# Linear-attention keys of layer 1 in memory of their own, projected and scored ahead of the state-space mixer's end

## The chip, the cores and the metric

The kernel runs on one core of one Trainium2 chip, in one launch. The metric is the device time of one execution in microseconds (us), the median of several runs. In the profile PE is the tensor engine, DVE the vector engine, ACT the scalar engine, POOL the general engine and SP the engine whose queue issues the DMAs.

## The reference, cut to what matters

Two layers of a hybrid backbone act on 512 latent tokens and 256 context tokens (768 together, width 1024). In each layer a normalised input is projected once, and the result is cut into four head groups: A, a chunked gating MLP; B, bidirectional gated linear attention; C, a bidirectional state-space mixer (S5); D, latent attention with rotary positions. Their outputs are joined and projected back, and a gated feed-forward block follows. Only the latent tokens leave layer 1, so there the context rows matter only as keys, values and states.

Group B is the one whose work is moved:

```
q, k, v, g = rs(q), rs(k), rs(v), rs(g)          # chunks of 64 tokens
cum = jnp.cumsum(g, axis=2)
q_in = q * jnp.exp(cum)
k_in = k * jnp.exp(-cum)
scores = jnp.where(tri, einsum('bcthk,bcshk->bchts', q_in, k_in), 0.0)
o_intra = einsum('bchts,bcshv->bcthv', scores, v)
s_fin, s_start = lax.scan(step, s0, (decay, kv_chunk))   # state from chunk to chunk
o_inter = einsum('bcthk,bchkv->bcthv', q_in, s_start)
out = rmsnorm(o_intra + o_inter, g_norm) * silu(r)
```

## The kernel before, in words

Tokens lie along the free axis, features along the partitions. A float32 product is made of three matmuls on a high and a low part of each operand (`mm3`, lines 199 to 201). A weight block of 512 KB is loaded as `raw`, then ACT makes its high part `whi` (L191) and DVE its low part `wlo` (L192). The order on each engine is set by a scheduler that goes over the program; each engine works its own list off in order, and SP issues the DMAs in order too.

`mixers` writes one layer's mixers. The state-space mixer (`mixer_c`, lines 680 to 818) runs in a memory pool `mc`, and projections of the other groups run beside it, two at a time, in the accumulators `pg`; `evac` copies them out on ACT (L1536 for the latent part, L1538 for the context part). `heads` (L1565ff) projects q or k in two halves ("half 0", "half 1") and copies each head to the other 64 partitions by a DMA within the on-chip memory (L1572).

A pool's memory is given out as a stack. The keys (`bk`, 128 x 4 x 768) and the gate `r` (`rt`) live in pool `mb`, which is opened after `mc` is closed and so lies in `mc`'s memory: the first write of a key waits for the state-space mixer's last reader (L818).

`mixer_b` is a generator with stations: the gates (L845 to L868), the scaling of q (L873, L874), then in one station the scaling of k (L878 on ACT, L879 on DVE), six blocks of transposes of k (L885 on PE, copied by L886 on ACT), the scores (L897 on PE, masked by L901 and L902 on DVE), the state scan of 12 steps (L922 on PE, L929 to L932 on DVE, L912 and L913 on ACT) and the outputs (L944 to L957). Latent attention (`mixer_d`) follows with a rotated key part (L1088 on PE, which needs the table `dcst` loaded by L1068), values (L1097), projections (L1109, L1121) and attention.

In the state-space mixer of layer 1 the last part is: 96 matmuls in four groups (L786, L788) on 32 KB tables `s5t` (L680) and `s5e` (L781), copies (L789), a gelu (L792), transposes (L798), copies (L800), the gate product (L814, L816 to L818) and the store of its output (`dmixr<-s5a`, L1552).

Of the kernel before, what the change touches and what calls it, by code (L numbers as in the profile page):

```python
# [15 lines left out]
ALU = mybir.AluOpType  # L16
# [74 lines left out]
class Net:  # L91
# [730 lines left out]
    def mixer_b(self, l, e, gl, pg, psp, ctx_out):  # L822
# [14 lines left out]
        tmp = self.t(pg, [128, 2, T], "bsc")  # L837
# [3 lines left out]
        for hp in range(2):  # L841
            for h in (2 * hp, 2 * hp + 1):
                ps = self.t(self.psp, [128, 1024], p2)
# [3 lines left out]
                b = self.col(l, "bgate", h)  # L847
# [23 lines left out]
        tmp = self.t(pg, [128, 2, T], "bsc")  # L871
# [1 line left out]
            nc.scalar.activation(tmp[:, h % 2, :tn], gates[:, h, :tn], AF.Exp, scale=1.0 / 16)  # L873
            stt(qd[:, h, :tn], qd[:, h, :tn], 0.125, tmp[:, h % 2, :tn], op0=ALU.mult, op1=ALU.mult)  # L874
        yield
        p, kd, vt = e.p, e.k, e.v
        for h in range(4):
            nc.scalar.activation(tmp[:, h % 2], gates[:, h], AF.Exp, scale=-1.0 / 16)  # L878
            tt(kd[:, h], kd[:, h], tmp[:, h % 2], op=ALU.mult)  # L879

        ktok = self.t(pg, [128, 6, 4, 128], "bg")
        for i in (4, 5, 0, 3, 1, 2):
            ps = self.t(self.psp, [128, 512], p1)
            for h in range(4):
                nc.tensor.transpose(ps[:, h * 128:(h + 1) * 128], kd[:, h, i * 128:(i + 1) * 128], self.ident)  # L885
            nc.scalar.copy(ktok[:, i].rearrange("p h c -> p (h c)"), ps[:])  # L886


# [1 line left out]
        for i in range(0, ni, 2):  # L890
            ps = self.t(self.psp, [128, 2, 2, 4, 64], p2)
            for d in range(2):
                for j in range(2):
                    for h in range(4):
                        for cp in range(2):
                            cs = slice((i + j) * 128 + cp * 64, (i + j) * 128 + cp * 64 + 64)
                            nc.tensor.matmul(ps[cp * 64:cp * 64 + 64, d, j, h, :], kd[d * 64:d * 64 + 64, h, cs],  # L897
                                             qd[d * 64:d * 64 + 64, h, cs], start=True, stop=True)
            m2 = self.m2.unsqueeze(1).to_broadcast([128, 8, 64])
            scv = sc[:, i:i + 2].rearrange("p i h t -> p (i h) t")  # L900
            tt(scv, ps[:, 0].rearrange("p j h t -> p (j h) t"), m2, op=ALU.mult)  # L901
            nc.vector.copy_predicated(scv, self.mgt[:], ps[:, 1].rearrange("p j h t -> p (j h) t"))  # L902

        sh = self.t(p, [128, 12, 4, 64], "bk")
        nc.gpsimd.memset(sh[0:64, 8], 0.0)
# [2 lines left out]
        for k in range(12):  # L908
# [7 lines left out]
            if k % 2 == 0:  # L916
                ps = self.t(self.psp, [128, 512], p1)
            o = k % 2 * 256
            for d, c in ((0, c0), (1, c1)):
                cp = (c % 2) * 64  # L920
# [17 lines left out]
        for i0 in range(0, ni, 2):  # L938
            ps = self.t(self.psp, [128, 512], p1)
# [6 lines left out]
            for o, i, h, cp in blocks:  # L946
                c = 2 * i + cp
# [7 lines left out]
        rs = self.rsqrt_dve(p, ss[:, :4 * ni], 4 * ni, 1.0 / 64, "br")  # L955
# [3 lines left out]
        rt = e.r  # L959
# [4 lines left out]
        for hp in range(2):  # L964
# [3 lines left out]
            ps = self.t(self.psp, [128, 1024], p2)  # L968
# [542 lines left out]
    def mixers(self, l, ctx, md, early=None):  # L1511
        nc = self.nc
        G = (0, 1, 2) if ctx else (0, 1)
        G3 = (0, 1, 2)
        tn = T if ctx else NX
# [5 lines left out]
        def fm(wv, groups):  # L1521
            px = pc = None
            if 0 in groups:
                px = self.t(self.psg, [128, 512], "pg")
                self.gemm_fm(wv, KT, self.hrhs, px, None, [g for g in groups if g < 2])
            if 2 in groups:
                pc = self.t(self.psg, [128, 512], "pg")
                self.gemm_fm(wv, KT, self.hrhs, None, pc[:, :256], [2])
            return px, pc


        def half(n, i):
# [18 lines left out]
        def store(o, k, mix, t0=0):  # L1551
            nc.sync.dma_start(md[:, o + k, t0:tn], mix[:, t0:tn])  # L1552
# [9 lines left out]
        px_ = mxs.__enter__()  # L1562
        env = SimpleNamespace()

        def heads(n, x, groups):
            w = 256 * len(groups)
            for hp in range(2):
                px, pc = fm(half(n, hp), groups)
                for hr in range(2):
                    rs = slice(hr * 64, hr * 64 + 64)  # L1570
                    evac(x[rs, 2 * hp + hr], px, pc, rs)
                    nc.sync.dma_start(x[64 - hr * 64:128 - hr * 64, 2 * hp + hr, :w], x[rs, 2 * hp + hr, :w])  # L1572

        rest = iter(())

        def visit(n):
            for _ in range(n):
                next(rest, None)

        with self.pool("mc") as pm:  # L1580
            with self.behind(self.hlast if tables else None):
                for _ in tables or ():
                    pass
            self.mixer_c(l, self.uf[l], lambda k, t: store(4, k, t), pm, pcp, "pc1", ctx)
            if l == 0:
                rest = chain(*(self.mod_pair(p, self.gate) for p in (1, 2)))
            visit(2)
            x12 = self.t(px_, [128, 4, T], "x12")
            x6 = self.t(px_, [128, 1536], "x6")
            ut = x12[:, 0:2]  # L1590
            va = x12[:, 2:4].rearrange("p a t -> p (a t)").rearrange("p (i c) -> p i c", i=6)
            for i in range(2):
                px, pc = fm(half("ua", i), G)
                evac(ut[:, i], px, pc, func=AF.Gelu_apprx_tanh)
                visit(1)
            tmajor("va", G, lambda g, ps: nc.scalar.activation(
                va[:, 2 * g:2 * g + 2].rearrange("p i c -> p (i c)"), ps[:], AF.Gelu_apprx_tanh))
            visit(2)
            self.mixer_a(l, ut, va, x6, px_, "pb2", ctx)
            visit(2)  # L1600
            for k in range(2):
                store(0, k, ut[:, k])
            for i in range(2):
                px, pc = fm(half("cq", i), G3 if i else G)
                evac(cq[:, i], px, pc)
                visit(1)
            px, pc = fm(half("ck", 0), G3)
            evac(ck, px, pc)
            visit(2)
            if tabs:  # L1610
                tabs.__exit__(None, None, None)
            mgs = self.pool("mg", side="right")
            pg = mgs.__enter__()
            b = self.mixer_b(l, env, cq[:, 1], pg, ("pb2", "pb1"), ctx)
            next(b)
            visit(2)
            self.latent_norms(l, cq, ck, pg, "pb2", "pb1", ctx)
            visit(4)
            env.q = self.t(px_, [128, 4, T], "x12")
            heads("q", env.q, G)  # L1620
            next(b)
            env.v = vb = self.t(px_, [128, 6, 256], "x6")
            tmajor("vb", G3, lambda g, ps: nc.scalar.copy(
                vb[:, 2 * g:2 * g + 2].rearrange("p i c -> p (i c)"), ps[:]))
        pcs.__exit__(None, None, None)
        with self.pool("mb") as env.p:
            env.k = self.t(env.p, [128, 4, T], "bk")
            env.r = rt = self.t(env.p, [128, 2, T], "rt")
            heads("k", env.k, G3)
            next(b)  # L1630
            for hp in range(2):
                px, pc = fm(half("r", hp), G)
                evac(rt[:, hp], px, pc)
            next(b, None)
            for k in range(2):
                store(2, k, rt[:, k])
            psgs.__exit__(None, None, None)
            self.pe = None
            psds = self.pool("psd", space=PSUM, side="right")
            mds = self.pool("md", side="right")  # L1640
            pd, psd = mds.__enter__(), psds.__enter__()
            self.psd = {2: [(psd, "pd2")], 1: [(psd, "pd1")]}
            d = self.mixer_d(l, cq, ck, lambda k, t, t0: store(6, k, t, t0), pd, pg, ctx)
            next(d)
        mxs.__exit__(None, None, None)
        psls.__exit__(None, None, None)
        with self.pool("pse", space=PSUM) as pse, self.pool("me") as self.pe:
# [159 lines left out]
```

## Time and profile before

| | |
|---|---|
| three runs | 1907.22, 1909.77, 1914.28 us |
| median | 1909.77 us |
| the profiled execution's own time | 1912.24 us |
| span of the profile | 1910.4 us |
| mean granted clock of PE | 0.944 of full speed |
| PE busy | 1775.8 us (93%) |
| DVE busy | 1197.7 us (63%) |
| ACT busy | 776.7 us (41%) |
| POOL busy | 123.9 us (6%) |

The busy shares are averages over stages with different limits, so they say only that PE is the engine most in use. The time scale of all rows below is us from the start of the span. Layer 1's mixers take from about 1180 to 1450 of it, its feed-forward block what follows. "Idle before <- X" on a row is the time in which the engine waited for X. The clock is a share of 2.4 GHz: 1.00 is that level, 0.50 is 1.2 GHz, and values between are stretches with both.

### The profile page before, as it was taken

The numbers are of one execution on the slowest core, as the hardware profiler recorded it, in microseconds if no ns is written. First come the engines' busy times: TensorE is split into PE (matmuls) and PEld (weight loads), VectorE is DVE, ScalarE is ACT, GpSimd is POOL, SyncE is SP. The second block draws the span as 40 slices with busy tenths as digits, with TensorE's granted clock in tenths as the row PEclk, the third lists the DMA queues.
The fourth block names the chain that finished last, engine by engine and source line by source line (L and its number), as shares of the span: only waits on it lengthen the run. The fifth ranks groups of instructions, "written<-read, shape, count | busy, mean of one in ns | idle before, by whom it ended". The sixth has DMA issues, their size and how long they took to land.

```text
span 1910.4 us, 28205 instructions
## 1 busy us (share of the span) xinstructions
PE 1775.8 (93%) x11256; PEld 1515.4 (79%) x11256; DVE 1197.7 (63%) x2200; ACT 776.7 (41%) x1242; POOL 123.9 (6%) x142
## 2 busy tenths in 40 slices
PE   5899989899989899999999988997989999999996
PEld 2785677679977788888888886886668988888886
DVE  8866734664879853554885775683565765455555
ACT  2433454454753333322322344364444653333332
POOL 0000000000430000000000033000000310000002
PEclk7999998899999999999999988998889899999998
DMA  9457630015623342222564433323102523323341
GB/s 351 140 170 253 200 95 24 28 37 185 204 70 112 109 122 78 88 89 85 183 185 133 143 100 104 115 69 95 33 24 94 187 83 88 110 78 110 86 146 45
DMA packets 94386, 222.14 MB, mean 116 GB/s; under 512 B 10928, under 2 KB 41008, under 8 KB 93232
## 3 DMA queue, kind: packets, MB, share of 16 engines
q1 hardware_dynamic: 94256, 220.36, 37.0%
q8 instruction: 88, 1.44, 0.3%
q14 instruction: 42, 0.34, 0.1%
HBM read 193.35 MB, written 24.08 MB: 114 GB/s over the span
## 4 chain that ended last, share of the span: by engine, by line
PE 71%; DVE 11%; issue 9%; ACT 4%; DMA 2%; POOL 1%; SPq 0%; POOLq 0%; DVEq 0%; ACTq 0%
PE pf L199 16%; PE pf L200 16%; PE pf L201 16%; PE pg L199 3%; PE pg L201 3%; PE pg L200 3%; PE pb L243 1%; DVE wlo L192 1%; PE pd L1161 1%; PE pn L322 1%; DVE z L1215 1%; PE pc L714 1%; ACT whi L191 1%; DMA bk<-bk 1%; DVE nu L389 1%
## 5 line engine op out<-in xcount | busy, mean ns | idle before, releaser
L192 DVE TENSOR_TENSOR wlo<-raw,whi 128x1024 fp32r<-128x1024 f32 (+1 forms) x215 | 252.5, 1175 | 292.4 <-ACT whi L191 289.5
L191 ACT ACTIVATE whi<-raw 128x1024 fp32r<-128x1024 f32 (+1 forms) x215 | 217.4, 1011 | 398.0 <-PE pf L200 340.7
L199 PE MATMUL pf<-hhx,whi 128*128 128x512 f32 (+1 forms) x1032 | 365.8, 360 | 13.3 <-DVE z L1215 6.0
L200 PE MATMUL pf<-hlx,whi 128*128 128x512 f32 (+1 forms) x1032 | 369.1, 359 | 6.1 <-DVE hlx L391 5.9
L201 PE MATMUL pf<-hhx,wlo 128*128 128x512 f32 (+1 forms) x1032 | 366.8, 357 | 0.7 <-DVE wlo L192 0.5
L199 PEld LDWEIGHTS pf<-hhx,whi 128*128 128x128 f32 x1032 | 199.9, 196 | 41.2 <-issue 7.3
L200 PEld LDWEIGHTS pf<-hlx,whi 128*128 128x128 f32 x1032 | 201.8, 196 | 33.6 <-DVE hlx L391 8.9
L201 PEld LDWEIGHTS pf<-hhx,wlo 128*128 128x128 f32 x1032 | 201.8, 196 | 27.0 <-DVE wlo L192 1.5
L199 PE MATMUL pf<-g,whi 128*128 128x512 f32 (+1 forms) x552 | 185.8, 342 | 5.3 <-DVE z L1215 2.9
L201 PE MATMUL pf<-g,wlo 128*128 128x512 f32 (+1 forms) x552 | 187.5, 341 | 0.8 <-DVE wlo L192 0.8
L200 PE MATMUL pf<-g,whi 128*128 128x512 f32 (+1 forms) x552 | 187.8, 341 | 0.0
L1215 DVE SCALAR_TENSOR_TENSOR z<-pf,cols,z 128x511 f32<-128x511 f32 (+1 forms) x264 | 167.9, 656 | 28.3 <-ACT z L1213 25.8
L200 PE MATMUL pf<-hl,whi 128*128 128x256 f32 x432 | 123.0, 286 | 0.4 <-DVE hl L391 0.4
L199 PE MATMUL pf<-hh,whi 128*128 128x256 f32 x432 | 121.5, 286 | 1.6 <-ACT hh L390 1.5
L201 PE MATMUL pf<-hh,wlo 128*128 128x256 f32 x432 | 122.1, 284 | 0.0
L199 PEld LDWEIGHTS pf<-g,whi 128*128 128x128 f32 x552 | 104.7, 192 | 18.8 <-issue 3.7
L201 PEld LDWEIGHTS pf<-g,wlo 128*128 128x128 f32 x552 | 105.8, 192 | 12.2 <-DVE wlo L192 1.0
L200 PEld LDWEIGHTS pf<-g,whi 128*128 128x128 f32 x552 | 105.8, 192 | 11.5 <-DVE g L1265 0.2
L1213 ACT ACTIVATE z<-pf,cols 128x512 f32<-128x512 f32 (+1 forms) x132 | 90.1, 695 | 38.3 <-PE pf L201 29.9
L1294 DVE TENSOR_TENSOR y<-y,pf 128x512 f32<-128x512 f32 (+1 forms) x88 | 44.7, 515 | 73.1 <-PE pf L201 73.1
L125 POOL TENSOR_TENSOR nroy<-nroy,mhalf 128x2 f32<-128x2 f32 x10 | 10.0, 996 | 1202.4 <-DVE nroy L124 894.3
L199 PEld LDWEIGHTS pf<-hh,whi 128*128 128x128 f32 x432 | 82.4, 193 | 3.9 <-ACT hh L390 2.3
(465 smaller groups left out, 3408.5 us busy)
## 6 DMA issues: line engine op xcount, KB each, us to landing
raw<-in_w SPq DMA_DIRECT2D x170, 512.0 KB, 3.5
rawm<-in_wmod SPq DMA_DIRECT2D x64, 512.0 KB, 4.3
raw<-in_w SPq DMA_DIRECT2D x48, 384.0 KB, 3.2
wm<-in_wmod SPq DMA_DIRECT2D x8, 1024.0 KB, 10.4
silu<-in_wmod SPq DMA_DIRECT2D x16, 512.0 KB, 5.6
dx<-g SPq DMA_DIRECT2D x32, 256.0 KB, 2.3
dG<-gt SPq DMA_DIRECT2D x16, 256.0 KB, 2.8
dE<-es SPq DMA_DIRECT2D x16, 256.0 KB, 2.3
```

What stands on the lines that cost most here:

```text
L191: nc.scalar.activation(hv, src, AF.Copy)
L192: nc.vector.tensor_tensor(lv, src, hv.bitcast(F32), op=ALU.subtract)
L199: self.nc.tensor.matmul(out, lh, rh, start=i == 0, stop=False)
L200: self.nc.tensor.matmul(out, lh, rl, start=False, stop=False)
L201: self.nc.tensor.matmul(out, ll, rh, start=False, stop=i == n - 1)
L243: self.nc.tensor.matmul(acc[32 * q:32 * q + 2, :], self.ct[:, k, :], halves[q // 2][:, q % 2 * 512:q % 2 * 512 + 512], start=k == 0, stop= ...
L322: self.nc.tensor.matmul(ps[:, j:j + 1], acc[:, k, j * 128:(j + 1) * 128], self.ones[:, 0:1], start=k == 0, stop=k == 1)
L389: nc.vector.scalar_tensor_tensor(u[:], xk, sc, pb, op0=ALU.mult, op1=ALU.mult)
L714: nc.tensor.matmul(ps[:, g * NCH:(g + 1) * NCH], E[:, b * 4 + g, :], U[:, gg, :], start=True, stop=True)
L1213: nc.scalar.activation(z[:, o:o + m], p[:, :m], AF.Identity, bias=b, scale=w1)
L1215: self.last = nc.vector.scalar_tensor_tensor(z[:, o + d:o + d + m - 1], p[:, s:s + m - 1], w, z[:, o + d:o + d + m - 1], op0=ALU.mult, op1 ...
L1294: nc.vector.tensor_tensor(y[:, m, t0:t0 + tw], y[:, m, t0:t0 + tw], ps[:, :tw], op=ALU.add)
```

## The change

In layer 1 alone the keys become four tiles: two in the long-lived tiles `silu0` and `silu1`, which serve the modulation at the program's start and are not read in layer 1, and two in a new pool `mk` (128 x 2 x 768, 6 KB a partition) that is opened before `mc`. The tile `x12` shrinks in layer 1 to the 512 latent tokens, which pays for `mk`. The call that projects k stands before pool `mc` is closed, and `mixer_b` has one station more, behind the scores, so that scaling, transposes and scores of k are written ahead of pool `mb`. Within `mb`, `rt` comes before `bk` in both layers. Layer 0 keeps its order of instructions. Nothing is computed in another way: the counts of matmuls, copies and DMAs stay.

```diff
         yield
-        p, kd, vt = e.p, e.k, e.v
+        kd, vt = e.k, e.v
...
             nc.vector.copy_predicated(scv, self.mgt[:], ps[:, 1].rearrange("p j h t -> p (j h) t"))
+        yield
+        p = e.p
 
         sh = self.t(p, [128, 12, 4, 64], "bk")
...
+        k4, mks = None, None
+        if l:
+            mks = self.pool("mk")
+            mk = self.t(mks.__enter__(), [128, 2, T], "mk")
+            k4 = [self.t(self.cp, [128, D], f"silu{w}")[:, :T] for w in range(2)] + [mk[:, 0], mk[:, 1]]
         with self.pool("mc") as pm:
...
-            x12 = self.t(px_, [128, 4, T], "x12")
+            x12 = self.t(px_, [128, 4, tn], "x12")
...
+            if l:
+
+                env.k = lambda i: k4[i]
+                heads("k", env.k, G3)
+                next(b)
         pcs.__exit__(None, None, None)
         with self.pool("mb") as env.p:
-            env.k = self.t(env.p, [128, 4, T], "bk")
-            env.r = rt = self.t(env.p, [128, 2, T], "rt")
-            heads("k", env.k, G3)
+            env.r = rt = self.t(env.p, [128, 2, tn], "rt")
+            if l == 0:
+                kt = self.t(env.p, [128, 4, T], "bk")
+                env.k = lambda i: kt[:, i]
+                heads("k", env.k, G3)
+                next(b)
             next(b)
```

Lines behind the edits have other numbers in the changed kernel: 1 or 2 more in `mixer_b` and `mixer_d` from the scan on (L922 becomes L924, L1088 becomes L1090), L1536 becomes L1538, L1538 becomes L1540.

Three places show how the engines' lists move; the numbers behind a name tell one use of a tile from another.

**SP**, behind the prefetched weight blocks (`raw`): the tables of the state-space mixer's third and fourth group of matmuls (`s5t`, `s5e`) and what is issued around them. Before:

```order
L680 DMA s5t_10992<-dK_20_93 16x4x128
L781 DMA s5e_10990<-dG_18_91 128x2x512
L680 DMA s5t_10992<-dK_20_93 16x4x128 x7
L781 DMA s5e_11015<-dG_18_91 128x2x512
L680 DMA s5t_11017<-dK_20_93 16x4x128 x8
L173 DMA raw_13030<-in_w 128x1024
L118 DMA s5e_11066<-in_sm 128x512
L1552 DMA dmixr_96<-s5a_11068 128x512 x2
L1068 DMA dcst_12370<-in_cst 128x640
```

and now:

```order
L1575 DMA silu_1547_10724<-silu_1547_10724 64x768
L1575 DMA silu_1548_10725<-silu_1548_10725 64x768
L173 DMA raw_13036<-in_w 128x1024
L680 DMA s5t_10998<-dK_20_93 16x4x128
L781 DMA s5e_10996<-dG_18_91 128x2x512
L680 DMA s5t_10998<-dK_20_93 16x4x128 x7
L781 DMA s5e_11021<-dG_18_91 128x2x512
L680 DMA s5t_11023<-dK_20_93 16x4x128 x8
L118 DMA s5e_11072<-in_sm 128x512
L1575 DMA mk_10723<-mk_10723 64x768 x2
```

The head duplicates of the first two key tiles (`silu_1547`, `silu_1548`) and the weight block `raw_13036` (before `raw_13030`, behind the tables) now stand ahead of the tables. The duplicates of the other two key tiles, four rows of `bk` before, follow behind the tables, ahead of the store of the state-space mixer's output.

**ACT**, around the copies of the state-space mixer's transposes (L800) and the exponentials for q (L873) and for k (L878). Before:

```order
L800 COPY s5u_11041<-pc_1586_11042 128x96x4
L873 ACTIVATE bsc_11621<-bg_11454 128x512
L800 COPY s5u_11041<-pc_1587_11048 128x96x4
L873 ACTIVATE bsc_11621<-bg_11454 128x512
L800 COPY s5u_11041<-pc_1588_11054 128x96x4
L878 ACTIVATE bsc_11621<-bg_11454 128x768
L800 COPY s5u_11041<-pc_1589_11060 128x96x4
L878 ACTIVATE bsc_11621<-bg_11454 128x768
L816 ACTIVATE s5a_11068<-pc_1593_11071,s5hb_11069 128x512
L816 ACTIVATE s5a_11068<-pc_1594_11078,s5hb_11069 128x512
L1536 ACTIVATE bk_11798<-pg_11806 64x512
L1538 ACTIVATE bk_11798<-pg_11831 64x256
```

and now:

```order
L873 ACTIVATE bsc_11627<-bg_11460 128x512 x4
L191 ACTIVATE whi_13105<-raw_13032 128x1024
L878 ACTIVATE bsc_11627<-bg_11460 128x768 x2
L800 COPY s5u_11047<-pc_1589_11048 128x96x4
L800 COPY s5u_11047<-pc_1590_11054 128x96x4
L878 ACTIVATE bsc_11627<-bg_11460 128x768 x2
L800 COPY s5u_11047<-pc_1591_11060 128x96x4
L800 COPY s5u_11047<-pc_1592_11066 128x96x4
L886 COPY bg_11931<-pb_1682_11932 128x512
L886 COPY bg_11931<-pb_1683_11938 128x512
L191 ACTIVATE whi_13135<-raw_13034 128x1024
```

All four exponentials for k and one weight split (L191) now stand ahead of or between the copies L800, and the first copies of k's transposes (L886) right behind them; the copies of k out of the accumulators, which came behind L816, have gone to places ahead of these rows.

**PE**, at the start of the state scan (L922, now L924), with the last matmul of r's half 1 (`pg_12315`), transposes of k (L885), scores (L897) and the rotated key part (L1088, now L1090). Before:

```order
L201 MATMUL pg_12315<-hhx_3543,wlo_12312 128x512
L885 MATMUL pb_1685_11957<-cst_68,bk_11798 128x128 x4
L885 MATMUL pb_1686_11963<-cst_68,bk_11798 128x128 x4
L897 MATMUL pb_1689_12005<-x_1648_11550,bk_11798 64x64 x32
L922 MATMUL pb_1691_12043<-x_1658_11630,bg_11932 64x64 x8
L922 MATMUL pb_1694_12065<-x_1658_11630,bg_11932 64x64 x8
L1088 MATMUL pd_1736_12378<-ck_10707,dcst_12370 128x512
L1088 MATMUL pd_1736_12378<-ck_10707,dcst_12370 128x256
L922 MATMUL pb_1691_12043<-x_1658_11630,bg_11932 64x64 x8
L922 MATMUL pb_1697_12090<-x_1658_11630,bg_11932 64x64 x8
```

and now:

```order
L897 MATMUL pb_1689_11969<-x_1651_11556,silu_1547_10724 64x64
L897 MATMUL pb_1689_11969<-x_1651_11556,silu_1548_10725 64x64 x2
L897 MATMUL pb_1689_11969<-x_1651_11556,mk_10723 64x64 x4
L924 MATMUL pb_1693_12048<-x_1661_11636,bg_11931 64x64 x8
L924 MATMUL pb_1696_12070<-x_1661_11636,bg_11931 64x64 x8
L924 MATMUL pb_1693_12048<-x_1661_11636,bg_11931 64x64 x8
L1090 MATMUL pd_1738_12383<-ck_10707,dcst_12375 128x512
L1090 MATMUL pd_1738_12383<-ck_10707,dcst_12375 128x256
L897 MATMUL pb_1690_12004<-x_1651_11556,silu_1547_10724 64x64 x2
L897 MATMUL pb_1690_12004<-x_1651_11556,silu_1548_10725 64x64 x2
```

The scan's first matmuls follow directly on the first half of the scores; the second half (`pb_1690`) now comes behind the rotated key part, and one scan step more stands ahead of that part. All of r and of k's projection has left this place: half 1 of k begins where the state-space mixer's first group of matmuls (L788) stood, the rest of k and r lies between the groups and the transposes L798, and the last matmul of r's half 1 now stands one row ahead of the gate product L814.

## Rows read from the trace of the kernel before

**Rows 1.** The page, first line.

```profile
span 1910.4 us, 28205 instructions
```

**Rows 2.** Stretches of layer 1: busy time of each engine; columns in the first row.

```profile
core 0: us, PE busy (x) PEld busy (x) DVE busy (x) ACT busy (x) POOL busy (x), PEclk, DMA share, GB/s
1180.00:1281.00 101.00, 100.59 (x642) 87.77 (x641) 70.53 (x119) 41.91 (x62) 2.90 (x1) 1.00 0.35 102
1281.00:1321.00 40.00, 28.30 (x171) 24.92 (x171) 21.07 (x37) 24.99 (x36) 2.27 (x1) 0.83 0.25 74
1321.00:1353.00 32.00, 29.20 (x237) 23.82 (x238) 8.93 (x10) 11.08 (x17) 0.00 (x0) 0.89 0.31 93
1353.00:1394.00 41.00, 32.64 (x354) 22.63 (x349) 25.71 (x51) 15.63 (x31) 0.61 (x2) 0.78 0.05 14
1550.00:1600.00 50.00, 49.86 (x228) 41.25 (x227) 36.98 (x46) 27.93 (x36) 0.00 (x0) 1.00 0.36 103
```

**Rows 3.** PE in order of time: start, us, line, operation, [idle before].

```profile
1293.61 0.43 PE L786 MATMUL pc<-s5t,s5u 128*96 128x128 f32 x2 [3.47 <-DMA s5t<-dK]
...
1299.87 0.44 PE L786 MATMUL pc<-s5t,s5u 128*96 128x128 f32 x2
...
1302.11 0.60 PE L788 MATMUL pc<-s5e,s5a 128*96 128x128 f32 x4
...
1314.17 3.71 PE L814 MATMUL pc<-s5u,s5e 128*128 128x512 f32 x8
...
1320.02 0.50 PE L199 MATMUL pg<-hhx,whi 128*128 128x512 f32 x1 [1.25 <-ACT bk L1536]
...
1328.37 0.28 PE L201 MATMUL pg<-hh,wlo 128*128 128x256 f32 x1
...
1353.04 0.27 PE L922 MATMUL pb<-x,bg 64*64 64x64 f32 x1
...
1354.51 1.55 PE L1088 MATMUL pd<-ck,dcst 32*128 32x512 f32 x4
```

**Rows 4.** DVE in order of time, from 1285 to 1325.

```profile
1288.63 1.20 DVE L192 TENSOR_TENSOR wlo<-raw,whi 128x1024 fp32r<-128x1024 f32 x1
...
1289.93 0.95 DVE L859 TENSOR_TENSOR bsc<-bsc,bg 64x768 f32<-64x768 f32 x1
...
1320.29 0.68 DVE L818 TENSOR_TENSOR s5a<-s5a,s5u 128x512 f32<-128x512 f32 x1
```

**Rows 5.** ACT in order of time, behind L816.

```profile
1318.50 0.58 ACT L1536 ACTIVATE bk<-pg 64x512 f32<-64x512 f32 x1
```

**Rows 6.** PE by line, 1281 to 1353: count, busy us, mean ns, idle before.

```profile
L897 PE MATMUL pb<-x,bk 64*64 64x64 f32 x120 | 4.6, 224 | 0.0
L885 PE MATMUL pb<-cst,bk 128*128 128x128 f32 x24 | 4.0, 284 | 1.6 <-DVE bk L879 1.6
L145 PE MATMUL pb<-cst,dry 128*128 128x128 f32 x20 | 3.9, 365 | 0.0
...
L1039 PE MATMUL pb<-ones,bsc 96*128 96x1 f32 (+1 forms) x28 | 3.4, 245 | 1.1 <-ACT bsc L1037 1.1
L798 PE MATMUL pc<-cst,s5v 96*128 96x96 f32 x16 | 3.0, 345 | 3.8 <-ACT s5v L792 2.2 <-ACT s5u L800 1.6
```

**Rows 7.** SP's issues in order of time.

```profile
1287.55 0.33 SPq L680 DMA_DIRECT2D s5t<-dK  x1
...
1292.95 4.13 SPq L680 DMA_DIRECT2D s5t<-dK  x8
...
1318.10 3.23 SPq L1552 DMA_DIRECT2D dmixr<-s5a  x2
1323.14 0.33 SPq L1068 DMA_DIRECT2D dcst<-in_cst  x1
```

**Rows 8.** DMAs issued from 1285 to 1345: KB each, median us to landing.

```profile
bk<-bk SPq DMA_DIRECT2D x4, 192.0 KB, 3.7
...
dcst<-in_cst SPq DMA_DIRECT2D x1, 320.0 KB, 2.8
```

More of the change, by code (lines that the diff above doesn't have):

```diff
@@ L875, in mixer_b @@
         yield
-        p, kd, vt = e.p, e.k, e.v
+        kd, vt = e.k, e.v
         for h in range(4):
             nc.scalar.activation(tmp[:, h % 2], gates[:, h], AF.Exp, scale=-1.0 / 16)
-            tt(kd[:, h], kd[:, h], tmp[:, h % 2], op=ALU.mult)
+            tt(kd(h), kd(h), tmp[:, h % 2], op=ALU.mult)
         ktok = self.t(pg, [128, 6, 4, 128], "bg")
@@ L884, in mixer_b @@
             for h in range(4):
-                nc.tensor.transpose(ps[:, h * 128:(h + 1) * 128], kd[:, h, i * 128:(i + 1) * 128], self.ident)
+                nc.tensor.transpose(ps[:, h * 128:(h + 1) * 128], kd(h)[:, i * 128:(i + 1) * 128], self.ident)
             nc.scalar.copy(ktok[:, i].rearrange("p h c -> p (h c)"), ps[:])
@@ L896, in mixer_b @@
                             cs = slice((i + j) * 128 + cp * 64, (i + j) * 128 + cp * 64 + 64)
-                            nc.tensor.matmul(ps[cp * 64:cp * 64 + 64, d, j, h, :], kd[d * 64:d * 64 + 64, h, cs],
+                            nc.tensor.matmul(ps[cp * 64:cp * 64 + 64, d, j, h, :], kd(h)[d * 64:d * 64 + 64, cs],
                                              qd[d * 64:d * 64 + 64, h, cs], start=True, stop=True)
@@ L1570, in heads @@
                     rs = slice(hr * 64, hr * 64 + 64)
-                    evac(x[rs, 2 * hp + hr], px, pc, rs)
-                    nc.sync.dma_start(x[64 - hr * 64:128 - hr * 64, 2 * hp + hr, :w], x[rs, 2 * hp + hr, :w])
+                    xv = x(2 * hp + hr)
+                    evac(xv[rs], px, pc, rs)
+                    nc.sync.dma_start(xv[64 - hr * 64:128 - hr * 64, :w], xv[rs, :w])
         rest = iter(())
@@ L1587, in mixers @@
             visit(2)
-            x12 = self.t(px_, [128, 4, T], "x12")
+            x12 = self.t(px_, [128, 4, tn], "x12")
             x6 = self.t(px_, [128, 1536], "x6")
             ut = x12[:, 0:2]
-            va = x12[:, 2:4].rearrange("p a t -> p (a t)").rearrange("p (i c) -> p i c", i=6)
+            va = x12[:, 2:4].rearrange("p a t -> p (a t)").rearrange("p (i c) -> p i c", c=256)
             for i in range(2):
@@ L1618, in mixers @@
             visit(4)
-            env.q = self.t(px_, [128, 4, T], "x12")
-            heads("q", env.q, G)
+            env.q = self.t(px_, [128, 4, tn], "x12")
+            heads("q", lambda i: env.q[:, i], G)
             next(b)
@@ L1644, in mixers @@
             next(d)
+        if mks:
+            mks.__exit__(None, None, None)
         mxs.__exit__(None, None, None)
```

## The prediction

> **What bounds the kernel now.** I read the page first, then the stretches of layer 1, then the engines in order of time around the one place that the change touches.
>
> The stretches show where PE is short of work. Up to 1281 it is busy 100.59 of 101.00 us at a granted clock of 1.00; from 1281 to 1321 only 28.30 of 40.00 at 0.83, from 1321 to 1353 29.20 of 32.00 at 0.89, and from 1353 to 1394 32.64 of 41.00 at 0.78; later, in the feed-forward block, 49.86 of 50.00 [rows 2]. So from 1281 to 1394 PE waits for chains, and outside it is full: what this stretch gets shorter by, the whole kernel gets shorter by.
>
> The timeline tells which chain. The state-space mixer ends with L818, which starts at 1320.29 and takes 0.68, so at 1320.97 [rows 4]. Half 0 of k is taken out of its accumulators at 1318.50, behind that mixer's last activation on ACT [rows 5], and half 1 of k starts on PE at 1320.02 with the idle time in front put down to that copy, ends at 1328.37 + 0.28 = 1328.65 and is followed by r, transposes and scores; the state scan starts at 1353.04, the rotated key part at 1354.51 [rows 3]. Thus 1353.04 - 1320.97 = 32.1 us of B's preparation stand in a row behind the mixer's end, while beside the mixer PE lay idle for 40.00 - 28.30 = 11.7 us. The reader is to see these two figures: work in a row behind a wall, and a hole in front of it.
>
> **The change part by part.** Nothing is removed or added in number; all of it is moved, so each cost is a question of where.
>
> *PE's work ahead of the scan.* From 1281 on the new list of PE holds, up to the scan's first matmul:
> - half 1 of k, 8.6 us (1320.02 to 1328.65 [rows 3]). It has 24 matmuls with 512 columns and 24 with 256, so the 512s take two thirds, 5.75, the 256s 2.9.
> - both halves of r, 24 with 512 columns each: 11.5.
> - the mixer's four groups L786/L788. The fourth took 1302.11 + 0.60 - 1299.87 = 2.84 [rows 3]; four at that rate make 11.4.
> - L814, 8 with 512 columns: 8/24 of 5.75 = 1.9.
> - L1039 3.4, L798 3.0, L145 3.9, L885 4.0, and for the first half of the scores 64 of 120 records of L897's 4.6 = 2.5 [rows 6]: 16.8 at the clock of these stretches. At full clock times about 0.86 (the mean of 0.83 and 0.89): 14.4.
>
> Together 8.6 + 11.5 + 11.4 + 1.9 + 14.4 = 47.8. Without any idle time the scan would start at 1281 + 47.8 = 1328.8.
>
> *SP, the idle that stays.* The tables of the third group are first issued at 1287.55 [rows 7], and PE already waits 3.47 us for them, to 1293.61 [rows 3]. In the new list the duplicates of two key tiles and a weight block stand ahead of them. That block waits for the L192 that ends at 1288.63 + 1.20 = 1289.8 [rows 4]; one more L859 (0.95 [rows 4]) now stands ahead of it on DVE, so about 1290.9, and the tables go out at about 1291.3: 3.8 later, usable at 1297.4. By then PE has done 20 matmuls of k (4.8), groups 1 and 2 (5.7), 21 more of k (3.0) and some of L1039 (0.9), and stands at 1295.4: 2.0 us idle. The fourth group, now begun at 1299.87, may wait till 1303.7, where PE arrives at about 1302.5: up to 1.2 more. I take 2.6 in all; the scan then starts at 1281 + 50.4 = 1331.4, **21.6 earlier** than 1353.04.
>
> *ACT and DVE.* k's copies, a split and four exponentials now stand ahead of or between the copies L800, so the mixer's tail is later. While they run PE has matmuls of r in its list, so I cost this at nothing beyond the sum; should that cover be gone, each us of ACT there is one of the scan's.
>
> *The mixer's end and `dcst`.* L814 stands ahead of 16 of the 24 L885 and of all first scores, (2.7 + 2.5) x 0.86 = 4.5, so it ends at 1326.9; now it ends at 1314.17 + 3.71 = 1317.9 and L818 3.1 later [rows 3, 4]. The mixer thus ends at 1330.0, 9.0 later than now. The table `dcst` is issued at 1323.14, behind the store of the mixer's output, 2.2 after L818's end [rows 7], and lands 2.8 after issue [rows 8]: 1330.0 + 5.0 = 1335.0 for the rotated key part, **19.5 earlier** than 1354.51. It stands behind three steps of the scan where there were two; the second scores (4.6 - 2.5 = 2.1) come behind it. The one step more in hand and the scores that are late are of the same size, and I set them against each other.
>
> *The duplicates* took 3.7 us each to land [rows 8], with the chain behind them waiting; now they run while PE has k and r in hand: nothing on the path. Layer 0 keeps its order: nothing.
>
> The two paths give 21.6 and 19.5; I take 20, nearer to the later one, since latent attention waits for it. The profiled execution took 1912.24 (span 1910.4 [rows 1] and 1.8 around it), 2.5 above the median of 1909.77: 1912.2 - 20 = 1892.2, and against the median **1889.8**.
>
> *Both ends.* Best: no idle at all, scan at 1328.8, gain 24.2. Worst: PE keeps the busy time that it has now, 28.30 + 29.20 - 2.1 = 55.4 [rows 2], with the present wait of 3.5 on top: scan at 1281 + 58.9 = 1339.9, gain 13.1. I stand nearer to the best end, since k and r, 20.1 of the 47.8, are dense matmuls that PE can put where it now idles, as in the row up to 1281.
>
> **The rivals.**
>
> *The clock does not come back.* The sum takes the mixer's groups at the fourth group's rate and small matmuls at full clock. If PE runs them with the holes and the 0.83 to 0.89 of [rows 2], the gain is the worst end's 13.1: 1909.8 - 13.1 = **1896.7**. For it: idle time stays ahead of groups 3 and 4. Against: the row at 1.00 is the one that is full. By "TensorE: Matmul & The Clock Gate" of the Trainium skill (Part 1) the throttled state is the default and activity releases it; that is what rows 2 show, and by that rule alone the filled stretch would run as in the best end.
>
> *The tables land late as well as leave late.* Ahead of them now go 2 x 192 KB [rows 8] and one 512 KB block, 896 KB. From 1281 to 1321 the DMA engines moved 74 GB/s at a busy share of 0.25, so 296 GB/s while busy [rows 2]: 3.0 us. If the tables have to stand behind all of it, groups 3 and 4 wait 3.0 more, and the gain is 17: **1892.8**. By "DMA: Bandwidth & Descriptors" of the Trainium skill ("Two DMAs through the same engine are not ordered") descriptors of one queue start in order on each engine, which speaks for this case and against the change; no row here shows two such loads behind one another.
>
> *No change, **1909.8**:* what sets the start of attention is not the scan but something with a time of its own, as a weight block. Against: from 1353 to 1394 the DMA share is 0.05 [rows 2], nothing is being waited for there.
>
> *Slower.* SP works in order, and three weight blocks and two duplicates stand ahead of the store of the mixer's output and of `dcst`. Each block waits until an earlier one is split on DVE. If the third is not free until after 1354.51 - 2.8 - 2.2 = 1349.5, the rotated key part is later than now; 10 us beyond that it is **1920**. Against: PE works r off before L814, and with that the splits.
>
> *It does not do what it says, **1909.8**:* the key tiles take memory whose readers are late. Against: `silu` has no reader in layer 1, and `mk` is opened ahead of `mc`.
>
> **How the numbers follow.** Forecast 0.50, late tables 0.20, clock 0.16, no change 0.07, not as it says 0.03, slower 0.04. The two middle cases are also faster. 0.5% of 1909.8 is 9.5 us, about what a measurement of this kernel can tell from no change; below 1900.3 lie the first three cases but for a little of the third: faster 0.84, same 0.12, slower 0.04. The range takes in the best end with the spread of the runs (1909.8 - 24.2 - 2.6 = 1883) and the worst with it (1896.7 + 4.5 = 1901): 1883 to 1901.
>
> **What would show it.** Right: half 1 of k starts at about 1281 with no idle ahead; the mixer's L818 ends at 1328 to 1332; the scan starts at 1329 to 1333, the rotated key part at about 1335; everything from 1400 on stands 18 to 22 earlier. Wrong: L818 later than 1336, the third group idle for more than 5 us, or the clock from 1281 to 1331 at 0.9 or less. Should the scan start 21 earlier and the end not, the last step was wrong: another chain binds attention.

## The result and the profile after

The changed kernel took 1888.70 us (median of 4 runs, 1886.21 to 1891.79), the kernel before, run beside it, 1912.03 (4 runs, 1907.22 to 1918.70). The ratio is 0.9865, 95% interval 0.9832 to 0.9899: faster, by 23.3 us between the medians, clear of noise. The profiled execution took 1888.02. The first line of its page, and its line of busy time, beside [rows 1]:

```profile
span 1886.2 us, 28206 instructions
...
PE 1765.4 (94%) x11256; PEld 1507.5 (80%) x11256; DVE 1196.9 (63%) x2200; ACT 777.0 (41%) x1242; POOL 123.8 (7%) x142
```

The span is 24.2 shorter, and PE is still the engine most in use, busy 94% of it.

The stretches of layer 1 after the change, same columns as in [rows 2], answer to the rows there:

```profile
1180.00:1281.00 101.00, 100.59 (x638) 87.68 (x637) 70.25 (x118) 41.72 (x61) 2.90 (x1) 0.99 0.32 92
1281.00:1321.00 40.00, 36.13 (x234) 33.10 (x234) 20.71 (x35) 27.40 (x39) 2.27 (x1) 0.91 0.37 104
1321.00:1353.00 32.00, 31.50 (x345) 24.87 (x344) 19.95 (x34) 15.49 (x28) 0.61 (x2) 0.77 0.23 76
1353.00:1394.00 41.00, 34.95 (x285) 24.78 (x286) 28.04 (x54) 16.53 (x33) 0.00 (x0) 0.80 0.08 27
```

The hole in front of the wall is mostly filled: from 1281 to 1321 PE is busy 36.13 us where it was 28.30 [rows 2]. The rows from 1321 on now hold other work than before, since all of it moved forward.

PE in order of time, after the change, at the places of [rows 3]: half 1 of k, the two idle times ahead of the third group, the fourth group, L814, the scan's start and the rotated key part.

```profile
1281.43 0.40 PE L199 MATMUL pg<-hhx,whi 128*128 128x512 f32 x1
...
1296.02 2.27 PE L1041 MATMUL pb<-ones,bsc 96*128 96x1 f32 x16 [2.11 <-ACT bsc L1039]
1300.05 0.71 PE L786 MATMUL pc<-s5t,s5u 128*96 128x128 f32 x2 [1.76 <-DMA s5t<-dK]
...
1307.00 0.38 PE L786 MATMUL pc<-s5t,s5u 128*96 128x128 f32 x2
...
1325.09 3.59 PE L814 MATMUL pc<-s5u,s5e 128*128 128x512 f32 x8
...
1332.97 0.27 PE L924 MATMUL pb<-x,bg 64*64 64x64 f32 x1
...
1335.93 0.66 PE L1090 MATMUL pd<-ck,dcst 32*128 32x512 f32 x1 [0.49 <-DMA dcst<-in_cst]
```

Half 1 of k starts at 1281.43 with no idle time in front (1320.02 before), the mixer's L814 10.9 later than before, the scan 20.07 earlier (1353.04 to 1332.97), the rotated key part 18.58 earlier (1354.51 to 1335.93) [rows 3].

SP's issues after the change, beside [rows 7]:

```profile
1289.45 1.11 SPq L1575 DMA_DIRECT2D silu<-silu  x2
1291.55 0.33 SPq L173 DMA_DIRECT2D raw<-in_w  x1
1291.98 0.38 SPq L680 DMA_DIRECT2D s5t<-dK  x1
...
1299.23 4.07 SPq L680 DMA_DIRECT2D s5t<-dK  x8
...
1308.74 19.68 SPq L173 DMA_DIRECT2D raw<-in_w  x3
1329.15 1.80 SPq L1554 DMA_DIRECT2D dmixr<-s5a  x2
1333.09 0.33 SPq L1070 DMA_DIRECT2D dcst<-in_cst  x1
```

The duplicates and the weight block stand ahead of the tables, which go out 4.4 later than at 1287.55 [rows 7]. From the first table's issue to the third group's start it is 8.1 now (1291.98 to 1300.05), where it was 6.1 (1287.55 to 1293.61) [rows 3, 7].

**Counting from one anchor.** In the nine profiled executions of this study (before, after and seven experiments), layer 1's first copy of `s5v` (DVE L774) starts anywhere from 1275.63 to 1288.56, though the engines' lists of before and after are the same until 2.2 us ahead of it. All times below are counted from that copy, the anchor. "Mixer's end" is the end of the last L818; "end" is the span's, and the other columns are starts. The first out-norm is the first L322 on `nsao`.

| kernel | ratio to before (95%) | anchor | mixer's end (L818) | scan starts | rotated key part | last state step | attention's `pe` | first out-norm | end |
|---|---|---|---|---|---|---|---|---|---|
| before | 1 | 1281.71 | 39.3 | 71.3 | 72.8 | 99.8 | 118.4 | 212.0 | 628.7 |
| after | 0.9865 | 1281.97 | 48.6 | 51.0 | 54.0 | 77.6 | 96.8 | 189.3 | 604.2 |
| e1 memory only | 0.987 (0.9842 to 0.9899) | 1275.63 | 48.7 | 51.1 | 54.3 | 78.0 | 97.2 | 190.0 | 604.5 |
| e2 half 0 only | 0.996 (0.9942 to 0.9977) | 1288.56 | 44.4 | 68.5 | 73.2 | 94.5 | 113.7 | 207.9 | 625.2 |
| e3 tables first | 0.9873 (0.9847 to 0.9898) | 1282.07 | 46.0 | 48.4 | 51.6 | 76.1 | 95.0 | 188.5 | 604.2 |
| e4 filler in the scan | 0.9916 (0.9898 to 0.9934) | 1281.98 | 48.5 | 52.3 | 57.3 | 79.8 | 99.0 | 198.7 | 614.5 |
| e5 half of r in the scan | 0.9928 (0.9901 to 0.9956) | 1281.96 | 47.7 | 51.2 | 62.9 | 80.1 | 102.5 | 197.6 | 614.9 |
| e6 both | 0.9905 (0.9868 to 0.9941) | 1286.59 | 45.0 | 48.4 | 60.2 | 77.5 | 99.5 | 194.9 | 611.7 |
| e7 layout only | 1.0013 (0.9994 to 1.0033) | 1288.33 | 39.5 | 71.7 | 73.2 | 101.8 | 121.4 | 216.8 | 633.3 |

"Last state step" is the last L932 or L934 on DVE (`bst<-bst,bdec`), "`pe`" the first L199 (`pe<-hh,hhx`) of attention. By these columns the change gains 20.3 at the scan, 18.8 at the rotated key part, 22.2 at the last state step, 21.7 at `pe`, 22.7 at the out-norm and 24.5 at the end. From the out-norm to the end the nine take 414.5 to 417.3, so the last 1.8 of the 24.5 lie within what executions differ by.

### The profile page after: what moved, and what is told of

The parts are those of the page before. It is cut to its first block, busy times and chain, and to the rows that moved or that the text cites. A ratio compares the mean times of both kernels' runs of the same rounds, so it can differ in the third digit from the quotient of the medians.

```text
span 1886.2 us, 28206 instructions
## 1 busy us (share of the span) xinstructions
PE 1765.4 (94%) x11256; PEld 1507.5 (80%) x11256; DVE 1196.9 (63%) x2200; ACT 777.0 (41%) x1242; POOL 123.8 (7%) x142
## 4 chain that ended last, share of the span: by engine, by line
PE 77%; DVE 12%; ACT 4%; DMA 3%; issue 2%; POOL 1%; SPq 0%; POOLq 0%; DVEq 0%; ACTq 0%
PE pf L199 17%; PE pf L200 17%; PE pf L201 17%; PE pg L201 3%; PE pg L199 3%; PE pg L200 3%; PE pd L1163 2%; PE pb L243 1%; DVE wlo L192 1%; PE pb L924 1%; PE pd L1156 1%; DVE z L1217 1%; DMA bx<-in_sm 1%; PE pn L322 1%; PE pc L714 1%
## 5 line engine op out<-in xcount | busy, mean ns | idle before, releaser
L199 PE MATMUL pf<-hhx,whi 128*128 128x512 f32 (+1 forms) x1032 | 366.0, 361 | 14.2 <-DVE z L1217 6.8
L191 ACT ACTIVATE whi<-raw 128x1024 fp32r<-128x1024 f32 (+1 forms) x215 | 217.4, 1011 | 388.8 <-PE pf L200 340.7
L199 PEld LDWEIGHTS pf<-hhx,whi 128*128 128x128 f32 x1032 | 200.3, 197 | 42.4 <-issue 8.1
L199 PE MATMUL pf<-g,whi 128*128 128x512 f32 (+1 forms) x552 | 185.7, 342 | 5.3 <-DVE z L1217 2.9
L199 PE MATMUL pf<-hh,whi 128*128 128x256 f32 x432 | 121.7, 286 | 1.5 <-ACT hh L390 1.5
L199 PEld LDWEIGHTS pf<-g,whi 128*128 128x128 f32 x552 | 104.7, 192 | 18.7 <-issue 3.7
L199 PEld LDWEIGHTS pf<-hh,whi 128*128 128x128 f32 x432 | 82.7, 194 | 3.5 <-ACT hh L390 2.0
```

The costliest lines, as they stand in the source:

```text
L191: nc.scalar.activation(hv, src, AF.Copy)
L199: self.nc.tensor.matmul(out, lh, rh, start=i == 0, stop=False)
```

## The experiments

**e1: the memory without the moved call.** Layer 1's keys stay in `silu` and `mk`, but `heads("k")` is called at its old place.

```diff
-            if l:
-
-                env.k = lambda i: k4[i]
-                heads("k", env.k, G3)
-                next(b)
         pcs.__exit__(None, None, None)
...
-                heads("k", env.k, G3)
-                next(b)
+            else:
+                env.k = lambda i: k4[i]
+            heads("k", env.k, G3)
+            next(b)
```

> Edit: the keys have their tiles in silu and mk as in the change, but the call that projects k stands again behind the end of pool mc, and the scores have no earlier place in the program than the change's last edit gives them. Theory (memory is the whole change): every engine has the same list as in the changed kernel, so the ratio to the kernel before is that of the change, 0.983 to 0.990, and the scan starts within 1 us of 1333. Rival (the place of the call does a part): the scan starts 3 us or more later than 1333, ratio 0.991 or more.

Measured: 1889.96 us (1881.91 to 1894.06, 4 runs), ratio 0.987; scan at 51.1, `pe` at 97.2, each within 0.5 of the change. The order of instructions on every engine is the change's own. So the place of the call decides nothing here: the scheduler that orders the engines' lists starts k as soon as its memory allows.

**e7: the layout without the memory for k.** The opposite part: station, `x12` and `rt` as in the change, the keys in `bk` again.

```diff
...
-            mk = self.t(mks.__enter__(), [128, 2, T], "mk")
-            k4 = [self.t(self.cp, [128, D], f"silu{w}")[:, :T] for w in range(2)] + [mk[:, 0], mk[:, 1]]
...
+            kt = self.t(env.p, [128, 4, T], "bk")
+            env.k = lambda i: kt[:, i]
+            heads("k", env.k, G3)
+            next(b)
```

> Only the new station and the moved buffers, with layer 1's keys in their old buffer again, so that they still wait for the mixer: no part of the change's effect should be left. Theory A (memory of the keys is the whole change): ratio 0.998 to 1.002, mixer end, scan, attention within 1 us of before (39.3, 71.3, 111.8). Rival (moving x12 and rt, or the station, is worth something by itself): ratio below 0.996 or above 1.004, or the scan off by over 2 us.

Measured: 1918.34 us (1911.21 to 1923.41, 10 runs), ratio 1.0013 (0.9994 to 1.0033): no change. Mixer's end and scan are within 0.4 of before. `pe` is 3.0 later, more than the 1 us expected, with the same order of instructions as before; a stretch from each shows where. First before, then e7 (columns as in [rows 2]), both from 94 to 104 behind the anchor:

```profile
1375.71:1385.71 10.00, 8.11 (x157) 5.87 (x157) 6.08 (x11) 4.98 (x11) 0.00 (x0) 0.99 0.01 2
```

```profile
1382.33:1392.33 10.00, 10.00 (x80) 5.86 (x80) 5.97 (x11) 5.02 (x11) 0.00 (x0) 0.50 0.01 2
```

In both the clock had been 0.50 in the 10 us ahead. In one execution it came back there, in the other not: PE worked off 157 records in 8.11 us of the 10, in e7 only 80 in 10.00. e1 has the change's order of instructions and e7 that of the kernel before, and the two programs differ only in the memory of layer 1's keys: that memory is the cause of the whole gain.

**e2: memory for half of the keys.** The first two key tiles in `silu`, the other two in `bk`.

```diff
...
-            k4 = [self.t(self.cp, [128, D], f"silu{w}")[:, :T] for w in range(2)] + [mk[:, 0], mk[:, 1]]
+            k4 = [self.t(self.cp, [128, D], f"silu{w}")[:, :T] for w in range(2)]
...
+            kt = self.t(env.p, [128, 4, T], "bk")
+            env.k = lambda i: k4[i] if l and i < 2 else kt[:, i]
```

> Edit: only the first two key tiles lie in silu; the other two lie in bk in pool mb, behind the state-space mixer's memory, and mk is gone. Theory (each key tile that waits for the mixer's memory holds back what follows it): half 1's matmuls (8.6 us) move ahead of the mixer's end, but its copies, their duplicates, r (11.5 us) and most transposes stay behind it; with a mixer's end at about 1328 the scan starts at 1343 to 1348, 5 to 10 us earlier than before (1353), ratio 0.994 to 0.998. Rival (the last key decides alone): 0 to 2 us, ratio 0.999 or more. Rival (half 0 alone opens the way): as the change, 0.990 or less.

Measured: 1907.29 us (1901.79 to 1915.58, 10 runs), ratio 0.996, inside the expected 0.994 to 0.998; by the anchor it gains 2.9 at the scan, 4.8 at `pe` and 3.4 at the end. The 2.9 at the scan miss the expected 5 to 10. The wall stands again, in front of the other half. ACT, PE and DVE of e2 in order of time:

```profile
1331.04 0.69 ACT L816 ACTIVATE s5a<-pc,s5hb 128x512 f32<-128x512 f32 x1 [1.03 <-PE pc L814]
1331.62 0.58 ACT L1538 ACTIVATE bk<-pg 64x512 f32<-64x512 f32 x1
...
1333.14 0.50 PE L199 MATMUL pg<-hhx,whi 128*128 128x512 f32 x1 [1.54 <-ACT bk L1538]
1341.94 0.69 PE L885 MATMUL pb<-cst,bk 128*128 128x128 f32 x2 [2.36 <-DVE bk L879]
...
1340.92 1.83 DVE L879 TENSOR_TENSOR bk<-bk,bsc 128x768 f32<-128x768 f32 x2 [7.93 <-DMA bk<-bk]
```

The first copy into a key tile behind the wall (L1538) follows the mixer's last activation (L816) on ACT. It does not wait for L818, as the part ahead of the prediction has it: L818 ends only at 1332.91 here, and in the kernel before the first write, at 1318.50 [rows 5], also precedes L818, at 1320.29 [rows 4]. So in the kernel before the wall stands 2.5 us ahead of the mixer's end, from which the 32.1 us behind it were counted. PE of e2 then waits for these copies, and DVE waits 7.93 for the DMA that duplicates the heads. Half the memory buys 4.8 of the 21.7 at `pe`, less than a quarter, because what stays behind the wall is still a chain: copies, duplicates, scaling, transposes, scores. e2 also parts two columns that move the same way elsewhere: the rotated key part is 0.4 *later* than before, and `pe` 4.8 earlier.

**e3: the tables ahead of the duplicates.** On SP, the duplicates of the key tiles and the fourth out-weight block wait for the last table's issue.

```diff
-                nc.sync.dma_start(TB[s * 16:s * 16 + 16],
+                self.lk = nc.sync.dma_start(TB[s * 16:s * 16 + 16],
...
+                    with self.behind(self.lk if l and n == "k" else None):
+                        nc.sync.dma_start(xv[64 - hr * 64:128 - hr * 64, :w], xv[rs, :w])
...
+            if l:
+                with self.behind(self.lk):
+                    self.pre.append(self.load_w(l, ("out", 1), 1))
```

> Edit: on the DMA queue of SP the duplicates of the first two key tiles and the one weight block for the output projection go behind the tables of the third and fourth group, in layer 1. Nothing else moves. Theory (what stands ahead of the tables makes them late): they are issued at about 1288.5 to 1289 instead of 1292, the third group starts at 1296 to 1297 instead of 1300.05, the mixer's end and the scan come 2 to 3.5 us earlier, time 2 to 3 us below the change. Rival (PE has other work there anyway): the third group starts earlier, the scan less than 1 us earlier, time within 1 us of the change. Rival (the duplicates are now late themselves): L879 on the first key tiles later than 1320, no gain or a loss.

Measured: 1889.07 us (1881.68 to 1896.74, 6 runs), ratio 0.9873, the change's own within the intervals. SP of e3 in order of time:

```profile
1288.25 0.33 SPq L680 DMA_DIRECT2D s5t<-dK  x1
...
1293.82 4.08 SPq L680 DMA_DIRECT2D s5t<-dK  x8
1298.00 1.15 SPq L1576 DMA_DIRECT2D silu<-silu  x2
```

and PE of e3 ahead of the third group:

```profile
1296.12 2.25 PE L1041 MATMUL pb<-ones,bsc 96*128 96x1 f32 x16 [2.11 <-ACT bsc L1039]
1298.23 0.72 PE L786 MATMUL pc<-s5t,s5u 128*96 128x128 f32 x2
```

The tables go out 3.7 earlier than in the change, PE no longer waits for them, and mixer and scan come 2.6 earlier. The third group starts at 1298.23, not at the expected 1296 to 1297, because PE's wait for ACT stays. At the last state step 1.6 of the 2.6 is left, at `pe` 1.8, at the out-norm 0.8, at the end nothing. So the late tables do hold the scan back by 2.6 us. What that is worth at the end is not shown: the expected 2 to 3 us did not appear, but the ratio's interval is some 10 us wide, and before and e7, with one order of instructions, differ by 3.0 at `pe`.

**e4: more work for PE in the scan.** Four fp32 matmuls of 128 x 128, overwritten by the real ones, ahead of each of the scan's accumulators, 24 in all (two records each in the trace).

```diff
                 ps = self.t(self.psp, [128, 512], p1)
+                for _ in range(0 if ctx_out else NFILL):
+                    nc.tensor.matmul(ps[:, :128], qd[:, 0, :128], qd[:, 1, :128], start=True, stop=True)
```

> Edit: each of the six accumulators of layer 1's state scan first gets four matmuls of 128x128 on q whose result is overwritten by the scan's own. It adds 24 matmuls to the work and changes no result. Theory (from 1338 to 1370 PE is held to half its clock by a stretch of small matmuls, and dense ones raise it): the granted clock from 1333 to 1378 rises from 0.71 to 0.85 or more, 32 scan matmuls take 1.3 to 2.0 us instead of 2.57, and the time is 2 to 6 us below the change. Rival (the clock stays, or the chain of the scan binds and not PE): 24 times 0.22 to 0.43 us, 5 to 10 us more than the change.

Measured: 1897.65 us (1895.79 to 1899.72, 6 runs), ratio 0.9916: some 5 thousandths above the change's, whose interval it just touches; its fastest run is slower than every run of e1, which has the change's list. Stretches of the changed kernel (in the scan, at the start of attention, from `pe` to the out-norm), and the same of e4:

```profile
1346.00:1356.00 10.00, 10.00 (x76) 6.93 (x77) 3.40 (x8) 5.52 (x13) 0.00 (x0) 0.50 0.00 0
...
1386.00:1396.00 10.00, 10.00 (x75) 8.65 (x74) 6.59 (x14) 4.73 (x9) 0.00 (x0) 1.00 0.00 0
...
1378.74:1471.32 92.58, 89.85 (x688) 81.72 (x688) 54.27 (x96) 44.98 (x86) 0.00 (x0) 0.98 0.27 89
```

```profile
1346.00:1356.00 10.00, 8.83 (x82) 7.98 (x83) 4.05 (x9) 4.82 (x10) 0.00 (x0) 0.66 0.00 0
...
1386.00:1396.00 10.00, 10.00 (x34) 7.16 (x34) 3.41 (x9) 3.79 (x9) 0.00 (x0) 0.50 0.00 0
...
1380.94:1480.66 99.72, 96.97 (x687) 86.37 (x688) 54.67 (x96) 45.22 (x86) 0.00 (x0) 0.91 0.25 82
```

In the scan the clock rose as expected, from 0.72 to 0.92 over the 43 us from 1333 to 1376, and PE was busy 36.27 there instead of 37.63 in spite of the added matmuls. But the scan was not shorter (27.5 from start to last state step, 26.6 in the change). PE and DVE of the changed kernel, then PE of e4, show why:

```profile
1333.20 2.24 PE L924 MATMUL pb<-x,bg 64*64 64x64 f32 x45
...
1339.69 2.52 PE L924 MATMUL pb<-x,bg 64*64 64x64 f32 x32
1342.14 3.78 PE L1099 MATMUL pd<-wg,ck 96*128 96x256 f32 x8
...
1348.51 0.42 DVE L933 TENSOR_TENSOR bst<-pb,bst 128x256 f32<-128x256 f32 x1 [2.89 <-PE pb L924]
...
1353.02 0.42 DVE L933 TENSOR_TENSOR bst<-pb,bst 128x256 f32<-128x256 f32 x1 [2.64 <-PE pb L924]
```

```profile
1341.86 1.43 PE L927 MATMUL pb<-x,bg 64*64 64x64 f32 x32
1343.66 1.99 PE L1102 MATMUL pd<-wg,ck 96*128 96x256 f32 x8 [0.38 <-ACT brs L1095]
1347.17 1.16 PE L922 MATMUL pb<-x 128*128 128x128 f32 x8 [1.51 <-DVE bst L936]
```

In the change PE binds the scan: DVE's steps wait for its matmuls. In e4 these got shorter (32 state matmuls 1.43 to 2.28 instead of 2.52 to 2.57, the first eight of L1099 1.99 instead of 3.78), but the fillers (L922) took 1.16 to 1.91 at each accumulator, 7.7 in all, and one of them waited 1.51 for DVE to read the accumulator that it overwrites. What the clock gave back the fillers used up, so e4 does not show what the half clock costs the scan. The rival's time came true, but not its conditions. And the clock was low later, at the start of attention, where PE is the bound: from `pe` to the out-norm the same matmuls took 99.7 at 0.91 instead of 92.5 at 0.98. `pe` is 2.2 later and the out-norm 9.4. Why the clock was low there is not shown.

**e5 and e6: half of r in the scan.** The second half of r (24 matmuls with 512 columns; the expectation's 36 was wrong) goes behind the scan's first step on PE: in e5 alone, in e6 together with e3's edit.

```diff
+                    self.sc[k] = nc.tensor.matmul(ps[d * 64:d * 64 + 64, o + h * 64:o + h * 64 + 64],
...
+                with self.behind(self.sc[R_AT[hp]] if l and hp else None):
+                    px, pc = fm(half("r", hp), G)
```

> The change, with the second r half (layer 1's x36 or so long matmuls that stand between S5 group 4 and the scan, 1310.98 to about 1324.6 in the profile after) put behind the first step of the scan. Times are counted from the first s5v copy. Theory A (the S5 tables and the DVE steps behind them set the end of the mixer, TensorE's r half only fills their waits): mixer end and scan start stay within 1 us (48.6 and 51.0), and the r half comes on top of the scan, where TensorE was busy without a gap at half clock: kr some 10 us later, attention 3 to 10 us later, total ratio 0.988 to 0.992; granted clock in the scan window above 0.71, as with the fillers. Theory B (TensorE's own work ahead of the scan also sets the scan's start): mixer end and scan 3 to 10 us earlier, attention no later than in the change, ratio 0.983 to 0.987.

> The two edits together: S5 tables ahead of the silu duplicates in SP's queue, and the second r half behind the scan's first step. Theory A (tables first, then DVE): mixer end and scan as with tables first alone (46.0 and 48.4), attention later by the r half as in the run before. Theory B (with the tables early, TensorE is what the mixer's end waits for): mixer end and scan another 3 us or more earlier than tables first alone, 43 and 45, and the total below both, ratio 0.980 to 0.986.

Measured: e5 1898.63 us (1896.51 to 1908.15, 5 runs), ratio 0.9928; e6 1897.97 us (1890.77 to 1902.76, 4 runs), ratio 0.9905. The scan starts at 51.2 and 48.4, as it does in the change and in e3: theory A holds in both, with a total a little above its 0.988 to 0.992 in e5. e6's interval (0.9868 to 0.9941) overlaps the change's, so its loss rests on the trace. The r half came on top instead, 8.9 and 8.6 later at the rotated key part, 5.7 and 4.5 at `pe`. PE of e5 shows what takes its place ahead of the scan:

```profile
1319.72 0.93 PE L799 MATMUL pc<-cst,s5v 96*128 96x96 f32 x8 [2.36 <-ACT s5u L801]
1320.75 0.44 PE L886 MATMUL pb<-cst,silu 128*128 128x128 f32 x2
1321.21 5.40 PE L815 MATMUL pc<-s5u,s5e 128*128 128x512 f32 x8
```

PE waits 2.36 for ACT's copies of the mixer's transposes, and L815 (L814 in the change), behind that wait, takes 5.40 at a granted clock of 0.68 where it took 3.59 at 1.00. In the change the r half lies over these waits, for nothing. No version here is clear of the change on the faster side.

## Why the prediction was right

The forecast was 1889.8 us, the change measured 1888.70. That they lie within 1.1 us is in part luck: the forecast took a gain of 20 from 1909.77, and the kernel before, run beside the change, took 1912.03, so the measured gain is 23.3. The steps:

- **PE's list ahead of the scan: right as a list, and in its sum by misses that cancel.** The sum was 47.8 of work. From 1281 to 1333, the scan's start, PE is busy 48.13 of 52.00 at a granted clock of 0.93. By the rows from 1281.43 on, overlaps counted once, k and r took 19.8 (forecast 20.1), the mixer's four groups 12.3 (11.4), L814 3.4 (1.9) and the small matmuls 12.1 (14.4). For L814 the row of before already showed 3.71 [rows 3]. The third group ran behind the idle time, at a clock of 0.59 from 1296 to 1304.3, and took 4.9 where the fourth took 2.8.
- **The idle that stays: right in cause, too small.** Forecast 2.0 ahead of the third group, at most 1.2 ahead of the fourth, 2.6 together. Measured 2.11 for ACT's `bsc` and 1.76 for the tables, 3.87 in all; the fourth group did not wait. The tables came 2.65 later than forecast (1300.05, not 1297.4): issued 0.7 later, and 2.0 longer from first issue to use. That is the rival of the tables that land late, in part: it expected 3.0. The Trainium skill, "DMA: Bandwidth & Descriptors", section "Two DMAs through the same engine are not ordered", says that descriptors of one queue start in order on each engine; the 2.0 longer behind the larger loads agrees with that. So does e3, where the order is turned round and the wait is gone. Scan forecast 1331.4, measured 1332.97.
- **ACT and DVE at nothing: right around L800.** In the change PE has r's matmuls there. e5 took that cover away: PE then waits 2.36 for ACT, and the scan is not earlier for the 24 matmuls fewer. Ahead of the third group there was no cover: PE waits 2.11 for ACT, where it was 1.1 [rows 6]. In the change the tables come later still, so this cost nothing more; in e3 it is what stays.
- **The mixer's end and `dcst`: right, the mixer again by two misses.** Mixer forecast 1330.0, measured 1330.6: L814 ended at 1328.7, 1.8 later than forecast, and from there to L818's end it took 1.9 instead of 3.1. Rotated key part 1335.0 and 1335.93.
- **"I take 20, nearer to the later one, since latent attention waits for it": the step that failed.** Attention waits for the scan's end, and the rotated key part's start does not tell when that is. DVE before, then after, last state step and last gating product (L972, L974), for which `pe` waits:

```profile
1381.51 0.41 DVE L932 TENSOR_TENSOR bst<-bst,bdec 128x256 f32<-128x256 f32 x1
...
1399.35 0.75 DVE L972 SCALAR_TENSOR_TENSOR rt<-pb,bhg,rt 128x512 f32<-128x512 f32 x1 [1.21 <-PE pb L970]
```

```profile
1359.59 0.43 DVE L934 TENSOR_TENSOR bst<-bst,bdec 128x256 f32<-128x256 f32 x1
...
1377.95 0.74 DVE L974 SCALAR_TENSOR_TENSOR rt<-pb,bhg,rt 128x512 f32<-128x512 f32 x1
```

  From the last state step to `pe` it is 18.6 before, 19.2 after, and 19.0 to 19.7 in e1 to e4 and e7 (22 in e5 and e6; in e5 the second part of L1125, 3.73 us of PE, stands between the last gating matmul and `pe`). From the rotated key part to `pe` it is 45.6 before, 42.8 after, and 39.3 to 48.2 in the experiments. In e2 the rotated key part is 0.4 later than before, and `pe`, 19.2 behind the last state step, 4.8 earlier. The scan's own path, forecast at 21.6, was the one to take, and by it the forecast would have been 1909.8 - 21.6 = 1888.2. The scan started 1.6 later than that path said, but it took 26.6 to its last state step instead of 28.5, so 22.2 were gained there by the anchor, and 21.7 at `pe`. Of the 1.9, 1.3 are idle time of PE in the scan (1.78 before, 0.50 after), which was not forecast; that 21.7 is so near to 21.6 is luck too.
- **What came on top.** From `pe` to the out-norm it is 92.5 instead of 93.6, and from there to the end 1.8 less, inside the spread of executions; a cause for these is not claimed. Of the prediction's signs the last is missed by this: from 1400 on the profile stands 21.4 earlier at `pe`, but 22.4 at the out-norm and 24.2 at the end, not 18 to 22. The others came, the scan at 1332.97 at the edge of its 1329 to 1333.
- **The rivals.** The clock ahead of the scan came back (0.93), but for the third group. No change and "does not do what it says" are out by the result, and by e1 and e7. The slower one came nearer than its point of decision said: SP stood at the three weight blocks from 1308.74 for 19.68, to 1328.42, and issued the store of the mixer's output at 1329.15. A block that came free 0.7 later would have begun to hold the store back, and with it `dcst`, for which PE already waits 0.49. PE works in order and has eight of the scan's eleven steps behind the rotated key part, so they would have come later as well; no run here shows by how much.

## What to carry to other kernels

When a tile's memory makes a step wait, ask first for other memory: here that gave the whole gain, and the place of the call in the program added nothing. Look for what was written long ago and is no longer read. Give all of it: with half of the keys freed, less than a quarter of the gain came, since the other half's chain still stood behind the wall. To price such a change, list the bound engine's work between the hole and the wall's far side and add only the waits that stay, then follow the path that really ends last by its last releaser, not the one whose start is latest. A term that a row already prices is taken from that row, as L814 was not.

## What the runs showed of the hardware that was not expected

- **A PE without a gap at half clock.** From 1346 to 1356 of the changed kernel PE is busy 10.00 of 10.00, and the granted clock is 0.50, so the level of 1.2 GHz. Ahead of it ran matmuls of 64 x 64 (scores and state steps): 32 of L924 took 2.52 us from 1339.69 on, where 45 had taken 2.24 at 1333.20. The Trainium skill, "TensorE: Matmul & The Clock Gate", Part 1, says that activity releases the throttle. Here it was on while the profile shows PE busy without a gap, so the page alone would have put this stretch at the upper level; with e4's larger matmuls among the small ones the clock of the scan was higher.
- **The clock's return is part of the spread.** Of two executions with one order of instructions, before and e7, one had 0.99 and the other 0.50 in the same 10 us, and in the other `pe` was 3.0 later. An experiment at this place that moves less than that needs the timed runs, not one trace.
